# Half of a feed-forward's down-projection blocks computed with seven half-size products, and up and down work interleaved

## The chip, the cores and the metric

The kernel runs on one core of one Trainium2 chip. The metric is the device time of one execution in microseconds, from its first to its last instruction with the launch around it. Five engines run their own instruction streams and meet through semaphores: TensorE (PE in the profile, with PEld for the loads of its stationary operand), VectorE (DVE), ScalarE (ACT), GpSimd (POOL) and SyncE (SP), which only issues the DMAs.

## The reference

A two-layer decoder trunk on a sequence of 256 positions with model width 2048. Each layer has a mixer and then a dense feed-forward with hidden width 8192; the change touches only the two feed-forwards:

```python
def squared_relu_mlp(h, w_up, w_down):
    return jnp.square(jax.nn.relu(h @ w_up)) @ w_down
...
    for layer in range(DEPTH):
        ...
        y = squared_relu_mlp(rmsnorm(h, norm_w[layer, 2]), ffn_w_up[layer], ffn_w_down[layer])
        h = h + rmsnorm(y, norm_w[layer, 3])
```

All tensors are float32.

## The kernel before

**Three products for one.** Every operand is split into a rounded part and a remainder (`whi` and `wlo` for weights, `e0h` and `e0l` for hidden activations), and a product is the sum of three matmuls: high times high, low times high, high times low. A unit of weights is one DMA of 1 MB into a `raw` tile (128 partitions, 2048 columns: four 128-row tiles of 512 columns each). ScalarE then writes `whi` (line 122) and VectorE writes `wlo = raw - whi` (line 123). There are three `raw` buffers and four each of `whi` and `wlo`, so the preparation of a unit can run up to four units ahead of its use.

**A feed-forward.** The hidden width is cut into 16 chunks of 512. The function `first_chunk` computes chunk 0. For each chunk from 1 to 15, `up_pass` computes the hidden chunk transposed: four units, in each unit 48 matmuls with 256 moving columns, into two `tp` banks of PSUM (lines 315 to 317). ScalarE applies relu (line 332), GpSimd squares (line 333), and the result is split into `e` (lines 185 and 186). Then `down` multiplies the hidden chunk before it with the down weights, in four blocks of 512 output columns: per block one unit of weights and 24 matmuls with 512 moving columns, into two `acc` banks, one for each half of the 256 positions. VectorE adds the two banks to `y` in SBUF (line 238) after each block. The order on TensorE is thus four up units, then four down blocks. The last chunk's down projection is done by `down_last`, together with the norm and the residual.

**What sets the order.** The tile framework schedules the instructions onto each engine's queue when the kernel is built; on each engine the order is then fixed, and waits are on semaphores. PSUM has eight banks of 512 float32 columns: four `acc`, two `tp`, two `mx`.

Of the kernel before, what the change touches and what calls it, by code (L numbers as in the profile page):

```python
# [10 lines left out]
F32 = mybir.dt.float32  # L11
# [6 lines left out]
P = 128  # L18
# [13 lines left out]
AHEAD = 200  # L32

# [57 lines left out]
def program(tc, nc, A, S):  # L91
# [60 lines left out]
    def chunk_tok(s, X, rows, spans, n):  # L152
        ps = [bank(acc, n, "acc") for _ in range(2)]
        for u in range(0, len(rows), 4):
            w = weights(s, [(r, spans) for r in rows[u : u + 4]])
            for j in range(4):
                k = u + j
                for b in range(2):
                    prod_tok(ps[b], X[k], b, w, j, n, k == 0, k == len(rows) - 1)
                tick()  # L160
# [142 lines left out]
    def up_pass(s, X, c):  # L303

        ps = [bank(tpp, 512, "tp") for _ in range(2)]
# [13 lines left out]
        return ps  # L319

    def ffn(up, dn, X, rh, w1i, w0i):
        with tc.tile_pool(name=f"ffn{w1i}", bufs=1, reuse_waits="tile") as fp:

            def hidden(e, b, ps):
# [3 lines left out]
                blocks_split(T(fp, [P, 512], "tr", bufs=2), r, e, b)  # L328

            def hidden_t(e, i, ps):  # L330
                r = T(fp, [P, 512], "rl", bufs=3)
                ACT.activation(r, ps, AF.Relu)  # L332
                G.tensor_tensor(r, r, r, ALU.mult)  # L333
                sl = slice(2 * i, 2 * i + 2)
                split(e[0][:, sl, :], e[1][:, sl, :], r.rearrange("p (m t) -> p m t", t=SEQ))
# [4 lines left out]
            e = group(fp, "e0h", "e0l")  # L340
            for b, ps in first_chunk(up, X, [(0, 512)]):
                hidden(e, b, ps)
            for c in range(1, HID // 512):
                e2 = group(fp, f"e{c % 2}h", f"e{c % 2}l")
                ps = up_pass(up, X, c)
                for i in range(2):
                    hidden_t(e2, i, ps[i])
                down(dn, kts([e]), rows(c - 1), c == 1)
                e = e2
            w1 = row_load([T(fp, [P, 512], f"w1{c}") for c in range(4)], "nrow", w1i)  # L350
            w0 = None
            if w0i is not None:
                w0 = row_load([T(fp, [P, 512], f"w0{c}") for c in range(4)], "nrow", w0i)
            return down_last(dn, kts([e]), rows(HID // 512 - 1), w1, w0,
                             lambda b: [T(fp, [P, 512], f"yw{c}") for c in range(4)], rh)
# [662 lines left out]
```

## Time and profile before

| | |
|---|---|
| median of 3 runs (lowest to highest) | 2580.64 us (2579.50 to 2581.19) |
| the profiled execution | 2581.39 us, span 2579.6 us |
| mean granted TensorE clock | 0.996 |
| TensorE busy | 2544.0 us (99%) |
| VectorE, ScalarE, GpSimd busy | 1620.2 us (63%), 1075.3 us (42%), 302.2 us (12%) |
| DMA | 477.85 MB, 185 GB/s in the mean |

The span is the time between the first and the last instruction in the trace; the profiled execution's own time is 1.8 us longer, and 0.75 us above the median. A busy TensorE is not TensorE at its peak, since the recorded matmuls overlap in the pipeline; how far apart they start tells its pace.

### The profile page before, as it was taken

To read this page: it belongs to the slowest core of one execution; us is meant where nothing else is said; L and a number is where in the kernel's file an instruction comes from. 1 tells how busy PE (TensorE), PEld (TensorE's weight loads), DVE (VectorE), ACT (ScalarE), POOL (GpSimd) and SP (SyncE) were. 2 spreads that over 40 slices of the span, in tenths; PEclk is the share of its full clock that TensorE was granted. 3 is DMA by queue.
4 is the path that set the end of the run, shared out by engine and by line. 5 is a ranking of instruction groups with operands and counts; after the bars stand their busy time and mean duration, and the time that the engine had idled before them with its cause. 6 is when DMAs were issued, how large, how long until landed. Compare 5 with 4: busy or idle time off the path is not lost.

```text
span 2579.6 us, 33644 instructions
## 1 busy us (share of the span) xinstructions
PE 2544.0 (99%) x14058; PEld 2183.4 (85%) x14058; DVE 1620.2 (63%) x1774; ACT 1075.3 (42%) x1084; POOL 302.2 (12%) x222
## 2 busy tenths in 40 slices
PE   8999999999999999999999999999999999999998
PEld 7778888879899898989878877777798998989897
DVE  7586855576555656555654596876865555565655
ACT  6555444443434333343443333333534343333433
POOL 3001101140000000000310110110400000000001
PEclk9999999999999999999999999999999999999999
DMA  7544545656555555555455555555465555555553
GB/s 243 177 157 142 196 153 173 209 177 214 193 181 189 187 185 191 182 193 181 156 211 185 175 204 203 190 194 196 163 216 192 181 193 181 190 186 184 191 182 112
DMA packets 81241, 477.85 MB, mean 185 GB/s; under 512 B 13633, under 2 KB 15809, under 8 KB 26817
## 3 DMA queue, kind: packets, MB, share of 16 engines
q1 hardware_dynamic: 81088, 475.70, 53.7%
q8 instruction: 110, 1.80, 0.3%
q14 instruction: 43, 0.34, 0.0%
HBM read 473.04 MB, written 2.62 MB: 184 GB/s over the span
## 4 chain that ended last, share of the span: by engine, by line
PE 48%; DVE 2%; POOL 0%; issue 0%; DVEq 0%; POOLq 0%; ACT 0%; ACTq 0%
PE acc L131 11%; PE acc L129 11%; PE acc L130 11%; PE tp L315 4%; PE tp L316 4%; PE tp L317 4%; DVE h L271 1%; PE mx L928 0%; DVE wlo L123 0%; DVE bc L214 0%; DVE y L259 0%; POOL rs L181 0%; DVE xl L186 0%; POOL e L275 0%; POOL yw L275 0%
## 5 line engine op out<-in xcount | busy, mean ns | idle before, releaser
L123 DVE TENSOR_TENSOR wlo<-raw,whi 128x2048 fp32r<-128x2048 f32 (+2 forms) x440 | 1000.4, 2276 | 729.9 <-ACT whi L122 727.7
L122 ACT ACTIVATE whi<-raw 128x2048 fp32r<-128x2048 f32 (+2 forms) x440 | 828.4, 1883 | 1019.1 <-PE acc L130 604.7
L315 PE MATMUL tp<-xh,whi 128*128 128x256 f32 x1920 | 539.6, 281 | 0.0
L317 PE MATMUL tp<-xh,wlo 128*128 128x256 f32 x1920 | 539.4, 281 | 0.0
L316 PE MATMUL tp<-xl,whi 128*128 128x256 f32 x1920 | 539.4, 281 | 0.0
L129 PE MATMUL acc<-whi,xh 128*128 128x512 f32 (+3 forms) x1120 | 447.1, 399 | 6.1 <-ACT whi L122 6.1
L131 PE MATMUL acc<-wlo,xh 128*128 128x512 f32 (+3 forms) x1120 | 440.1, 393 | 8.6 <-DVE wlo L123 8.6
L130 PE MATMUL acc<-whi,xl 128*128 128x512 f32 (+3 forms) x1120 | 439.5, 392 | 0.0
L316 PEld LDWEIGHTS tp<-xl,whi 128*128 128x128 f32 x1920 | 361.8, 188 | 1.4
L315 PEld LDWEIGHTS tp<-xh,whi 128*128 128x128 f32 x1920 | 361.7, 188 | 1.4
L317 PEld LDWEIGHTS tp<-xh,wlo 128*128 128x128 f32 x1920 | 361.8, 188 | 0.0
L131 PEld LDWEIGHTS acc<-wlo,xh 128*128 128x128 f32 x1120 | 212.0, 189 | 57.3 <-DVE wlo L123 11.0
L129 PEld LDWEIGHTS acc<-whi,xh 128*128 128x128 f32 x1120 | 212.4, 190 | 52.3 <-ACT whi L122 7.0
L130 PEld LDWEIGHTS acc<-whi,xl 128*128 128x128 f32 x1120 | 212.6, 190 | 45.0 <-issue 1.0
L333 POOL TENSOR_TENSOR rl<-rl 128x512 f32<-128x512 f32 x60 | 95.5, 1592 | 1219.3 <-ACT rl L332 1139.1
L238 DVE TENSOR_TENSOR y<-acc,y 128x512 f32<-128x512 f32 x248 | 167.8, 689 | 72.6 <-PE acc L131 71.8
L130 PE MATMUL acc<-whi,e1l 128*128 128x512 f32 x512 | 202.3, 395 | 0.0
L131 PE MATMUL acc<-wlo,e1h 128*128 128x512 f32 x512 | 202.3, 395 | 0.0
L129 PE MATMUL acc<-whi,e1h 128*128 128x512 f32 x512 | 202.3, 395 | 0.0
L130 PE MATMUL acc<-whi,e0l 128*128 128x512 f32 x512 | 202.3, 395 | 0.0
L131 PE MATMUL acc<-wlo,e0h 128*128 128x512 f32 x512 | 202.2, 395 | 0.0
L129 PE MATMUL acc<-whi,e0h 128*128 128x512 f32 x512 | 202.2, 395 | 0.0
(268 smaller groups left out, 2464.7 us busy)
## 6 DMA issues: line engine op xcount, KB each, us to landing
raw<-up SPq DMA_DIRECT2D x128, 1024.0 KB, 4.9
raw<-dn SPq DMA_DIRECT2D x128, 1024.0 KB, 4.9
raw<-sg_in SPq DMA_DIRECT2D x64, 1024.0 KB, 5.0
raw<-la_in SPq DMA_DIRECT2D x56, 1024.0 KB, 5.0
raw<-sg_out SPq DMA_DIRECT2D x32, 1024.0 KB, 5.0
raw<-la_out SPq DMA_DIRECT2D x16, 1024.0 KB, 5.0
raw<-la_in SPq DMA_DIRECT2D x4, 768.0 KB, 4.3
w<-nrow SPq DMA_DIRECT2D x12, 256.0 KB, 5.8
```

Of the source, the lines that this page charges most:

```text
L122: ACT.activation(a, r, AF.Copy)
L123: V.tensor_tensor(d, r, a.bitcast(F32), ALU.subtract)
L129: PE.matmul(ps, xh, wh, start=first, stop=False)
L130: PE.matmul(ps, xl, wh, start=False, stop=False)
L131: PE.matmul(ps, xh, wl, start=False, stop=last)
L238: V.tensor_tensor(y[b][c], ps, y[b][c], ALU.add)
L271: V.scalar_tensor_tensor(ht, yb[c], rs, ht, ALU.mult, ALU.add)
L315: PE.matmul(out, wh[:, col], xh, start=k == 0 and m % 2 == 0, stop=False, skip_group_check=True)
L316: PE.matmul(out, wh[:, col], xl, start=False, stop=False, skip_group_check=True)
L317: PE.matmul(out, wl[:, col], xh, start=False, stop=k == NKT - 1, skip_group_check=True)
L333: G.tensor_tensor(r, r, r, ALU.mult)
```

## The change

**Seven products.** A down block multiplies a 256 x 512 matrix of hidden values by a 512 x 512 matrix of weights. In two of the four blocks (`SEVEN`, output columns 0 to 511 and 1024 to 1535) and for 15 of the 16 chunks, both matrices are cut into halves in each direction, and the product is formed by Winograd's variant of Strassen's scheme from seven products of halves in place of eight. A product of halves is six matmuls with 256 moving columns (two tiles of 128 rows, three matmuls each), so a block has 42 matmuls of 256 columns where it had 24 of 512. The stationary operand is a 128 x 128 tile of `e`, or of `f`, which holds sums and differences of halves of `e`; `sums` forms `f` once for each chunk. The weights' sums are formed by VectorE in `qsum` (four quarter matrices), and both `raw` and `qsum` are split, so such a block takes two `whi` and two `wlo` buffers. Its results fill two `acc` banks (`pa`, `pb`) and two `mx` banks (`pc`, and half of `pd`), each added to an accumulator of its own. `combine` turns the accumulators into `y` after the last such block.

**One block kept.** The block `KEPT` (columns 512 to 1023) accumulates over its 15 chunks in two `acc` banks and is copied out once; two `acc` banks are left for the other blocks.

**Alternation.** `up_pass` is now a generator that stops after each unit. `ORDER` puts one down block behind each up unit (`None` is an up unit); `FIRST` is the order for chunk 1. The rows of the norm weights are loaded into tiles of `f` and `e` that are no longer needed.

```diff
+SEVEN, KEPT = (0, 2), 1
+ORDER = (None, 0, None, 1, None, 2, None, 3)
+FIRST = (None, None, 1, None, 0, None, 3, 2)
...
-    def chunk_tok(s, X, rows, spans, n):
-        ps = [bank(acc, n, "acc") for _ in range(2)]
+    def chunk_tok(s, X, rows, spans, n, ps=None, first=True, last=True):
+        if ps is None:
+            ps = [bank(acc, n, "acc") for _ in range(2)]
...
-                    prod_tok(ps[b], X[k], b, w, j, n, k == 0, k == len(rows) - 1)
+                    prod_tok(ps[b], X[k], b, w, j, n, first and k == 0, last and k == len(rows) - 1)
...
-    def up_pass(s, X, c):
-
-        ps = [bank(tpp, 512, "tp") for _ in range(2)]
...
-        return ps
+            yield
+    def mul7(s, pool, rows, col):
+        H = 256
+        n1, n2 = [(col, H)], [(col + H, H)]
+        src, width = s.take([(rows[0], n2), (rows[1], n2), (rows[0], n1), (rows[1], n1),
+                             (rows[2], n2), (rows[3], n2), (rows[2], n1), (rows[3], n1)])
+        raw = T(wp, [P, 2048], "raw", bufs=RAW_BUFS)
+        q = T(pool, [P, 2048], "qsum")
+        hi = [T(wp, [P, 2048], "whi", F32R, bufs=HI_BUFS) for _ in range(2)]
+        lo = [T(wp, [P, 2048], "wlo", F32R, bufs=LO_BUFS) for _ in range(2)]
+        DMA.dma_start(raw, src)
+        B = raw.rearrange("p (q n) -> p q n", n=512)
+        Q = q.rearrange("p (q n) -> p q n", n=512)
+        V.tensor_tensor(Q[:, 0:2, :], B[:, 1:3, :], B[:, 0:1, :].to_broadcast([P, 2, 512]), ALU.add)
+        V.tensor_tensor(Q[:, 2, :], Q[:, 0, :], B[:, 2, :], ALU.add)
+        V.tensor_tensor(Q[:, 3, :], Q[:, 2, :], B[:, 3, :], ALU.add)
+        split(hi[0][:, :1536], lo[0][:, :1536], raw[:, 512:])
+        split(hi[1], lo[1], q)
+        return [[(t[0][:, k * 512 : (k + 1) * 512], t[1][:, k * 512 : (k + 1) * 512]) for k in range(n)]
+                for t, n in (((hi[0], lo[0]), 3), ((hi[1], lo[1]), 4))]
+    def chunk7(s, pool, e, f, rows, col):
+        (b11, b22, b21), (q1, q3, q2, q4) = mul7(s, pool, rows, col)
+        def plain(half, b):
+            return [[t[:, 2 * half + k, b * P : (b + 1) * P] for t in e] for k in range(2)]
+        def summed(i):
+            return [[t[:, i, k * P : (k + 1) * P] for t in f] for k in range(2)]
+        def prod(ps, x, w):
+            for k in range(2):
+                wh, wl = [t[:, k * 256 : (k + 1) * 256] for t in w]
+                PE.matmul(ps, x[k][0], wh, start=k == 0, stop=False, skip_group_check=True)
+                PE.matmul(ps, x[k][1], wh, start=False, stop=False, skip_group_check=True)
+                PE.matmul(ps, x[k][0], wl, start=False, stop=k == 1, skip_group_check=True)
+        R1, R2, R3, S4 = range(4)
+        pa, pd, pb, pc = bank(acc, 512, "acc"), bank(mxp, 256, "mx"), bank(acc, 512, "acc"), bank(mxp, 512, "mx")
+        prod(pa[:, :256], plain(0, 0), b11)
+        prod(pa[:, 256:], plain(1, 0), b21)
+        prod(pd, summed(S4), b22)
+        prod(pb[:, :256], summed(R2), q2)
+        prod(pb[:, 256:], summed(R3), q3)
+        prod(pc[:, :256], summed(R1), q1)
+        prod(pc[:, 256:], plain(1, 1), q4)
+        return pa, pb, pc, pd
...
+            def sums(a, c):
+                t = T(fp, [P, 1024], "tr")
+                F = t.rearrange("p (i m t) -> p i m t", m=2, t=P)
+                V.tensor_tensor(F[:, 0], a[1][0], a[1][1], ALU.subtract)
+                V.tensor_tensor(F[:, 1], F[:, 0], a[0][0], ALU.subtract)
+                V.tensor_tensor(F[:, 2], a[0][0], a[1][0], ALU.subtract)
+                V.tensor_tensor(F[:, 3], F[:, 1], a[0][1], ALU.add)
+                f = pair(f"f{c % 2}")
+                split(f[0].rearrange("p a t -> p (a t)"), f[1].rearrange("p a t -> p (a t)"), t)
+                return f
...
+            Y, kept = {}, [bank(acc, 512, "acc") for _ in range(2)]
+            def add(key, ps, first, n=512):
+                if first:
+                    Y[key] = T(hp, [P, 512], *BUF[key])[:, :n]
+                    V.tensor_copy(Y[key], ps)
+                else:
+                    V.tensor_tensor(Y[key], ps, Y[key], ALU.add)
...
+            def block(c, g, e, f):
+                if c in SEVEN:
+                    ps = chunk7(dn, fp, e, f, rows(g), c * 512)
+                    for k, p, n in zip("abcd", ps, (512, 512, 512, 256)):
+                        add((k, c), p, g == 0, n)
+                elif c == KEPT:
+                    chunk_tok(dn, kts([e]), rows(g), [(c * 512, 512)], 512, kept, g == 0, g == last - 1)
+                    if g == last - 1:
+                        for b in range(2):
+                            acc_to_y(kept[b], b, c, True)
+                else:
+                    for b, p in enumerate(chunk_tok(dn, kts([e]), rows(g), [(c * 512, 512)], 512)):
+                        acc_to_y(p, b, c, g == 0)
...
+            def combine(c):
+                a, b, p, p3 = [Y[k, c] for k in "abcd"]
+                u = T(fp, [P, 512], "rl", bufs=3)[:, :256]
+                l, r = slice(0, 256), slice(256, 512)
+                V.tensor_tensor(u, a[:, l], b[:, l], ALU.add)
+                V.tensor_tensor(a[:, l], a[:, l], a[:, r], ALU.add)
+                V.tensor_tensor(a[:, r], p[:, l], p3, ALU.add)
+                V.tensor_tensor(a[:, r], a[:, r], u, ALU.subtract)
+                V.tensor_tensor(u, u, b[:, r], ALU.add)
+                V.tensor_tensor(b[:, l], u, p[:, r], ALU.add)
+                V.tensor_tensor(b[:, r], p[:, l], u, ALU.subtract)
+                y[0][c], y[1][c] = a, b
...
-            for c in range(1, HID // 512):
-                e2 = group(fp, f"e{c % 2}h", f"e{c % 2}l")
-                ps = up_pass(up, X, c)
-                for i in range(2):
-                    hidden_t(e2, i, ps[i])
-                down(dn, kts([e]), rows(c - 1), c == 1)
-                e = e2
...
+            for c in range(1, last + 1):
+                e2 = pair(f"e{c % 2}")
+                if c == last:
+                    w1 = row_load(rows_in(["f1h", "f1l"]), "nrow", w1i)
+                ps = [bank(tpp, 512, "tp") for _ in range(2)]
+                todo = up_pass(up, X, c, ps)
+                order = ORDER if c > 1 else FIRST
+                for n, o in enumerate(order):
+                    if o is None:
+                        next(todo)
+                        if None not in order[n + 1 :]:
+                            r = [relu2(p) for p in ps]
+                            for i in range(2):
+                                sl = slice(2 * i, 2 * i + 2)
+                                split(e2[0][:, sl, :], e2[1][:, sl, :], r[i].rearrange("p (m t) -> p m t", t=SEQ))
+                            if c < last:
+                                a = [x.rearrange("p (m b t) -> p b m t", b=2, t=P) for x in r]
+                                f2 = sums([[a[i][:, b] for i in range(2)] for b in range(2)], c)
+                    else:
+                        block(o, c - 1, e, f)
+                e, f = e2, f2
+            for o in SEVEN:
+                combine(o)
```

**VectorE, around the end of an up pass, before.** `wlo` is a weight split, `e0l` the split of the new hidden chunk, `y` the add of a finished `acc` bank.

```order
L123 TENSOR_TENSOR wlo_5490<-raw_5488,whi_5489 128x2048
L186 TENSOR_TENSOR e0l_5155<-rl_5374,e0h_5154 128x512
L186 TENSOR_TENSOR e0l_5155<-rl_5379,e0h_5154 128x512
L238 TENSOR_TENSOR y_923_5042<-acc_5384,y_923_5042 128x512
L238 TENSOR_TENSOR y_924_5044<-acc_5385,y_924_5044 128x512
L123 TENSOR_TENSOR wlo_5526<-raw_5524,whi_5525 128x2048
L238 TENSOR_TENSOR y_930_5078<-acc_5418,y_930_5078 128x512
```

**The same place, now.** `qsum` rows form weight sums, `tr` rows form the sums that become `f`, and lines 190 and 126 are the splits.

```order
L341 TENSOR_TENSOR qsum_6153<-raw_6152 128x1024
L190 TENSOR_TENSOR wlo_6156<-raw_6152,whi_6154 128x1536
L342 TENSOR_TENSOR qsum_6153<-qsum_6153,raw_6152 128x512
L400 TENSOR_TENSOR tr_6051<-rl_6041 128x256
L190 TENSOR_TENSOR e1l_5664<-rl_6041,e1h_5663 128x512
L190 TENSOR_TENSOR e1l_5664<-rl_6044,e1h_5663 128x512
L398 TENSOR_TENSOR tr_6051<-rl_6041,rl_6044 128x256
L343 TENSOR_TENSOR qsum_6153<-qsum_6153,raw_6152 128x512
L399 TENSOR_TENSOR tr_6051<-tr_6051,rl_6041 128x256
L401 TENSOR_TENSOR tr_6051<-tr_6051,rl_6044 128x256
L242 TENSOR_TENSOR y_948_5160<-acc_6060,y_948_5160 128x512
L190 TENSOR_TENSOR wlo_6157<-qsum_6153,whi_6155 128x2048
```

Behind these follow the split `f1l`, the add of the second bank of the plain block (`y_949`) and the split for the next up unit. Between the splits of the hidden chunk and the next weight split there are now the sums for `f`, and the second half of a seven-product block's weights waits there too. The same 33 VectorE rows come for each of the middle chunks of both feed-forwards.

**TensorE, where the first down block of a feed-forward begins, before.** The whole of the up pass for chunk 1 stands ahead of it.

```order
L129 MATMUL acc_5010<-whi_5013,e0h_4612 128x512
L130 MATMUL acc_5010<-whi_5013,e0l_4613 128x512
L131 MATMUL acc_5010<-wlo_5014,e0h_4612 128x512
L129 MATMUL acc_5011<-whi_5013,e0h_4612 128x512
L130 MATMUL acc_5011<-whi_5013,e0l_4613 128x512
```

**TensorE in the same first round, now: the seven-product block that follows directly on a plain block.** The plain block used both free `acc` banks; `acc_5178` is this block's `pa`.

```order
L363 MATMUL mx_5181<-whi_5167,f0l_4788 128x256
L364 MATMUL mx_5181<-wlo_5169,f0h_4787 128x256
L362 MATMUL mx_5181<-whi_5167,f0h_4787 128x256
L362 MATMUL acc_5178<-whi_5166,e0h_4614 128x256
L363 MATMUL acc_5178<-whi_5166,e0l_4615 128x256
```

Ten matmuls into the two `mx` banks now stand between the end of the plain block and the first matmul that needs an emptied `acc` bank. In the later rounds an up unit stands between any two down blocks.

## Rows read from the trace of the kernel before

**Rows 1.** The page: span, TensorE, granted clock in 40 slices.

```profile
span 2579.6 us, 33644 instructions
...
PE 2544.0 (99%) x14058; PEld 2183.4 (85%) x14058; DVE 1620.2 (63%) x1774; ACT 1075.3 (42%) x1084; POOL 302.2 (12%) x222
...
PEclk9999999999999999999999999999999999999999
```

**Rows 2.** Windows, one hidden chunk: busy us (instructions) by engine, clock, DMA share, GB/s.

```profile
876.10:921.20 45.10, 45.10 (x290) 40.70 (x290) 25.74 (x18) 17.43 (x13) 3.19 (x2) 1.00 0.54 187
```

**Rows 3.** Timeline of TensorE over that chunk: start us, us, instruction; cut.

```profile
875.92 0.28 PE L317 MATMUL tp<-xh,wlo 128*128 128x256 f32 x1
876.04 0.39 PE L129 MATMUL acc<-whi,e0h 128*128 128x512 f32 x1
876.28 0.40 PE L130 MATMUL acc<-whi,e0l 128*128 128x512 f32 x1
...
898.21 0.39 PE L131 MATMUL acc<-wlo,e0h 128*128 128x512 f32 x1
898.44 0.28 PE L315 MATMUL tp<-xh,whi 128*128 128x256 f32 x1
...
921.16 0.39 PE L129 MATMUL acc<-whi,e1h 128*128 128x512 f32 x1
```

**Rows 4.** Groups by form, whole span: TensorE 256-wide matmuls and their loads.

```profile
L315 PE MATMUL tp<-xh,whi 128*128 128x256 f32 x1920 | 539.6, 281 | 0.0
...
L317 PEld LDWEIGHTS tp<-xh,wlo 128*128 128x128 f32 x1920 | 361.8, 188 | 0.0
```

**Rows 5.** Groups by form, VectorE: total us, mean ns, idle before.

```profile
L123 DVE TENSOR_TENSOR wlo<-raw,whi 128x2048 fp32r<-128x2048 f32 x424 | 976.1, 2304 | 725.0 <-ACT whi L122 723.6 <-PE acc L131 0.9
...
L123 DVE TENSOR_TENSOR wlo<-raw,whi 128x1024 fp32r<-128x1024 f32 x4 | 4.9, 1227 | 4.7 <-ACT whi L122 4.0 <-PE mx L676 0.7
...
L775 DVE TENSOR_TENSOR bc<-PT 128x256 f32<-128x256 f32 x8 | 3.4, 424 | 5.5 <-POOL PT L773 5.3
```

**Rows 6.** Groups by form, ScalarE.

```profile
L122 ACT ACTIVATE whi<-raw 128x2048 fp32r<-128x2048 f32 x424 | 811.4, 1914 | 1004.8 <-PE acc L130 600.1 <-PE tp L316 319.3 <-DMA raw<-sg_out 44.1
L332 ACT ACTIVATE rl<-tp 128x512 f32<-128x512 f32 x60 | 35.3, 588 | 94.4 <-PE tp L317 94.4
...
L185 ACT ACTIVATE e1h<-rl 128x512 fp32r<-128x512 f32 x32 | 19.9, 623 | 36.1 <-POOL rl L333 36.1
...
L122 ACT ACTIVATE whi<-raw 128x1536 fp32r<-128x1536 f32 x4 | 5.9, 1481 | 5.7 <-DMA raw<-la_in 5.7
...
L122 ACT ACTIVATE whi<-raw 128x1024 fp32r<-128x1024 f32 x4 | 4.2, 1056 | 4.6 <-PE acc L130 4.6
```

**Rows 7.** Timeline of VectorE around the end of an up pass.

```profile
742.71 2.29 DVE L123 TENSOR_TENSOR wlo<-raw,whi 128x2048 fp32r<-128x2048 f32 x1 [3.39 <-ACT whi L122]
744.92 1.53 DVE L186 TENSOR_TENSOR e0l<-rl,e0h 128x512 fp32r<-128x512 f32 x1
746.61 0.69 DVE L186 TENSOR_TENSOR e0l<-rl,e0h 128x512 fp32r<-128x512 f32 x1 [0.15 <-ACT e0h L185]
747.21 1.28 DVE L238 TENSOR_TENSOR y<-acc,y 128x512 f32<-128x512 f32 x2
748.41 2.29 DVE L123 TENSOR_TENSOR wlo<-raw,whi 128x2048 fp32r<-128x2048 f32 x1
```

**Rows 8.** Timeline of GpSimd at the same place.

```profile
740.85 1.04 POOL L333 TENSOR_TENSOR rl<-rl 128x512 f32<-128x512 f32 x1 [40.07 <-ACT rl L332]
743.76 2.15 POOL L333 TENSOR_TENSOR rl<-rl 128x512 f32<-128x512 f32 x1 [1.86 <-ACT rl L332]
```

**Rows 9.** Windows in the last stretch of the first feed-forward.

```profile
1260.00:1280.00 20.00, 18.74 (x85) 14.31 (x83) 13.32 (x20) 9.03 (x15) 8.99 (x8) 1.00 0.26 97
1280.00:1300.00 20.00, 19.23 (x88) 14.93 (x88) 19.26 (x24) 13.64 (x30) 14.76 (x7) 1.00 0.65 236
```

**Rows 10.** The page, DMA issues: count, size, us to landing.

```profile
raw<-dn SPq DMA_DIRECT2D x128, 1024.0 KB, 4.9
```

More of the change, by code (lines that the diff above doesn't have):

```diff
@@ L301, in program, with up_pass @@
     ALLK = [k * P for k in range(NKT)]
-    def up_pass(s, X, c):
-        ps = [bank(tpp, 512, "tp") for _ in range(2)]
+    def up_pass(s, X, c, ps):
         for u in range(4):
@@ L321, in ffn, with pair, relu2 @@
     def ffn(up, dn, X, rh, w1i, w0i):
+        last = HID // 512 - 1
         with tc.tile_pool(name=f"ffn{w1i}", bufs=1, reuse_waits="tile") as fp:
-            def hidden(e, b, ps):
+            def pair(name):
+                return T(fp, [P, 4, SEQ], f"{name}h", F32R), T(fp, [P, 4, SEQ], f"{name}l", F32R)
+            def relu2(ps):
                 r = T(fp, [P, 512], "rl", bufs=3)
@@ L327, in hidden, with rows_in @@
                 G.tensor_tensor(r, r, r, ALU.mult)
[L328 to L335, printed above, removed]
+                return r
+            def rows_in(tags):
+                t = [T(fp, [P, 2, 512], g) for g in tags]
+                return [t[0][:, 0], t[0][:, 1], t[1][:, 0], t[1][:, 1]]
@@ L337, in rows @@
             def rows(c):
                 return [c * 512 + j * P for j in range(4)]
-            e = group(fp, "e0h", "e0l")
-            for b, ps in first_chunk(up, X, [(0, 512)]):
-                hidden(e, b, ps)
-            for c in range(1, HID // 512):
-                e2 = group(fp, f"e{c % 2}h", f"e{c % 2}l")
-                ps = up_pass(up, X, c)
-                for i in range(2):
-                    hidden_t(e2, i, ps[i])
-                down(dn, kts([e]), rows(c - 1), c == 1)
-                e = e2
@@ L350, in ffn @@
[L350 to L355, printed above, removed]
+            Y, kept = {}, [bank(acc, 512, "acc") for _ in range(2)]
[5 more added lines that the diff above has]
+                    V.tensor_tensor(Y[key], ps, Y[key], ALU.add)
@@ new lines, in ffn @@
+            BUF = {("a", 0): ("y00",), ("b", 0): ("y10",), ("a", 2): ("y02",), ("b", 2): ("y12",)}
+            for c in SEVEN:
+                BUF["c", c] = BUF["d", c] = ("bc", F32, 4)
+            def block(c, g, e, f):
[11 more added lines that the diff above has]
+                        acc_to_y(p, b, c, g == 0)
@@ new lines, in halves_of @@
+            def halves_of(tiles):
+                return [[t[:, m] for m in range(2)] for t in tiles]
+            e = pair("e0")
+            t = [T(hp, [P, 512], "bc", bufs=4) for _ in range(2)]
+            for b, ps in first_chunk(up, X, [(0, 512)]):
+                blocks(t[b], relu2(ps))
+                sl = slice(b * P, (b + 1) * P)
+                split(e[0][:, :, sl], e[1][:, :, sl], t[b].rearrange("p (j c) -> p j c", c=P))
+            v = [a.rearrange("p (i m t) -> p i m t", i=2, t=P) for a in t]
@@ new lines, in ffn @@
+            f = sums([[v[b][:, i] for i in range(2)] for b in range(2)], 0)
+            for c in range(1, last + 1):
[19 more added lines that the diff above has]
+                e, f = e2, f2
@@ L357, in layer0_mixer @@
+            for o in SEVEN:
+                combine(o)
+            w0 = None if w0i is None else row_load(rows_in(["f0h", "f0l"]), "nrow", w0i)
+            return down_last(dn, kts([e]), rows(last), w1, w0, lambda b: rows_in(["e0h", "e0l"]), rh)
     def layer0_mixer():
```

## Prediction

> **What bounds the kernel now.** I read the page first: TensorE is busy for 2544.0 of 2579.6 us and its granted clock is in the top tenth in all 40 slices [rows 1], so the time follows the number and spacing of matmuls, and nothing else counts unless TensorE comes to wait for it. Then the windows, for one hidden chunk: TensorE busy 45.10 of 45.10 us, clock 1.00 (the 2.4 GHz level), VectorE 25.74, ScalarE 17.43, GpSimd 3.19 [rows 2]. Then TensorE's timeline over that chunk, by starts, since recorded matmuls overlap: the 96 down matmuls of 512 columns run from 876.04 to 898.44, 0.2333 us each; the 192 up matmuls of 256 columns from 898.44 to 921.16, 0.1183 us each [rows 3]. So a down block (24) takes 5.60 us, an up unit (48) 5.68, a chunk 45.12. Half the columns cost half the time although each matmul loads another stationary tile. The neighbours come last: VectorE's and ScalarE's durations [rows 5, 6] and what they do at the end of an up pass [rows 7, 8].
>
> **The products.** A seven-product block has 42 matmuls of 256 columns: 42 x 0.1183 = 4.97 us for 5.60, a saving of 0.63. Two such blocks, 15 chunks and two feed-forwards make 60: -37.8 us. The chunk becomes 43.85 us. Its matmuls are of the up pass's form (load per matmul, half a bank of PSUM), so I take that spacing; bounds for it stand under the rivals.
>
> **VectorE in a steady chunk.** Per operation I take start-to-start times. Measured: 2.21 for a 2048-column split, 0.60 for an add or a 512-column operation in sequence [rows 7]. For 1024 columns I take 1.15 (its duration is 1.227 [rows 5], and starts of the 2048 split lie 0.1 closer than its duration), for 1536 the mean, 1.68, for 256 columns 0.34 (between half of 0.60 and the 0.424 in [rows 5]). A chunk has 33 operations: eight 2048 splits 17.7, two 1536 splits 3.4, weight sums 2 x 1.15 + 4 x 0.60 = 4.7, adds of the four results 6 x 0.60 + 2 x 0.34 = 4.3, the plain block's adds 1.2, splits of `e` 0.60 + 1.53 = 2.1, four `tr` 1.4, split of `f` 1.15. Sum 35.9 of 43.85 us: 82%, no bound. The trace has no weight sum from a repeated operand and no strided `tr`; from below they cost what I took, from above twice that, as an `e0l` split did once (1.53 against 0.69 [rows 7]): +6.1 per chunk, kept for a rival. ScalarE adds two splits of 1481, a net none of 1914 and one of 1056 ns [rows 6] to its 17.43, about 21.5: covered. Every unit is still one 1 MB DMA, which lands in 4.9 us [rows 10] with three `raw` buffers and units 5.5 us apart: nothing.
>
> **Where a chunk could wait.** The narrow place is the end of an up pass: `e` and `f` of the new chunk must be ready by the next chunk's first seven-product block, and the sums for `f` stand in VectorE's queue ahead of that block's second weight split, the add that frees a bank and the next unit's split. Let 0 be the end of the last up unit. TensorE runs the plain block to 5.60, an up unit to 11.28, then the seven-product block, whose 13th matmul (12.7) is the first to need `f`; its 19th (13.4) needs the bank of `y_949`; the next up unit begins at 16.25.
> VectorE's walk starts when block 2's `pa` is full, at -9.1: add 0.60, split 2.21, adds 0.60, 0.34 and 0.60, split 2.21, `qsum` 1.15, 1536 split 1.68, to +0.3; then `qsum` to 0.9. ScalarE's two relus (0.588 each [rows 6]) end at 0.1 and 0.7. The two squares take 1.04 us alone and 2.15 beside VectorE [rows 8]; at 2.15 each they end at 2.25 and 4.4. `e1h` of the second half (0.623 [rows 6]) ends at 5.0, its `e1l` at 5.6; three `tr` and one `qsum` reach 7.2, the add `y_948` 7.85. ScalarE meanwhile splits `qsum` from 6.6 to 8.5 (1.914), VectorE its remainder to 10.7, then `f1l` to 11.85, `y_949` 12.45, the next unit's split 14.65. Slack is 0.9, 1.0 and 1.6 us. After its backlog VectorE comes to the next `pa` at about 31.6 and waits for it until 34.8, so no lateness carries over: 0 for the 28 such boundaries.
>
> **First round.** Here block 2 follows directly on block 3, which filled both free `acc` banks; ten matmuls cover 1.2 us, so the first bank must be copied out by 5.60 + 1.2 = 6.8 after the up pass. VectorE, from that point: `qsum` to 0.25, squares at 1.2 to 2.25, `tr` and `qsum` to 3.8, a unit's split 6.0, splits of `e` 7.2, `tr` 7.55, copy 8.2. Stall about 1.5, twice: +3.0. Both ends: 0 if the copies are early, 3 each if the squares run at 2.15.
>
> **End.** `combine` is 14 operations, some 5 us of VectorE by 0.34 to 0.42 each, while the last blocks run; the last hidden split is now covered by one block (5.60) where it had four (22.4), and should be ready at 4 to 5.6, needed at 7.0. The old trace already lets TensorE wait there: 18.74 and 19.23 busy of 20 [rows 9]. Nothing to 6 us each; I take 0.5, hence +1.0, because the walk has it in time.
>
> **Sum.** 2581.4 (the profiled execution) - 37.8 + 3.0 + 1.0 = 2547.6; that execution is 0.75 above the median, so 2547 us.
>
> **Rivals.**
> *A wait at the boundary takes back the gain.* The slack of 0.9 us is 4% of a chain of 21 us of VectorE and GpSimd work. For it: every price but the measured ones is interpolated, and the squares and VectorE disturb one another (1.04 to 2.15, 0.69 to 1.53 [rows 7, 8]). Against: I already pay 2.15 for both squares. Each us beyond the slack costs 28 us: 1 us gives 2575. The Trainium skill, page "SBUF — State Buffer", section "Who interferes with whom", says that a VectorE instruction with two SBUF inputs and a GpSimd instruction that reads SBUF shut each other out for its whole length; the trace's two doublings agree. By that rule each square would end earlier or later by where it falls between splits, and my estimate for `f1l` is 10.8 in place of 11.85: the same sum. Chance 0.12.
>
> *VectorE becomes the bound: slower.* The repeated, strided and summing operations cost twice my price, +6.1 us per chunk; 3.2 of it goes into the wait before `pa`, 2.9 stalls TensorE at each boundary: 2547 + 28 x 2.9 = 2628. It decides from +4.4 per chunk, 1.7 times the price (3.2, and 33.8 us of gain over 28). For it: the 1.53 us split. Against: its neighbour of the same form took 0.69 [rows 7], and duration follows columns from 424 ns to 2304 [rows 5]. Chance 0.04.
>
> *Seven products are no saving.* If a product's matmuls went at the pace of their loads, 188 ns [rows 4], a block would take 7.90 us, +2.30 x 60 = +138: 2547 + 38 + 138 = about 2723. Against: the up pass has the same load for each matmul and starts one every 0.118 [rows 3]. The Trainium skill, page "TensorE: Matmul & The Clock Gate", section "Back-to-back issue gap", gives for steady pairs of load and matmul about 81 ns at 128 columns and 131 at 512, so half-width matmuls would cost more than half. My estimate by it, with 98 ns at 256: a block 1.31 times as long, 7.33 us, +104 in all, 2689. This trace shows 0.2333 and 0.1183, a ratio of 1.97, which decides. Chance 0.02.
>
> **How the numbers follow.** The forecast, no stall but in the first round, has 0.80: 2543 (no first-round or end cost: 2581.4 - 37.8 - 0.75) to 2556. The boundary wait has 0.12, the bound on VectorE 0.04, the load pace 0.02, anything else 0.02. What a measurement of this kernel can tell from no change is about 0.2%, 5 us: 2575.5 to 2585.8. The boundary wait stays faster up to 1.0 us of stall (28.5 over 28), which I give half its chance; the rest is split between same and slower. Faster 0.86, same 0.05, slower 0.09. The range for 8 in 10 runs from 2542 to 2568: below, a little for the end's old waits going; above, the end's 6 us each or a boundary stall of 0.7 us.
>
> **What would show it.** In the profile after: down matmuls of lines 362 to 364 starting 0.118 apart, a steady chunk of 43.85 us from one first `pa` matmul to the next, TensorE without idle time between; a hole of 1 to 2 us once per feed-forward after ten matmuls into `mx`; VectorE about 36 us per chunk with a wait of some 3 us ahead of the `pa` add; the weight sums near 1.2 (1024) and 0.6 us. I am wrong on the products if the pitch is above 0.118 or the clock below 1.00; on the boundary if idle time stands before the 13th or 19th matmul of block 0, released by `f1l` or `y_949`; on VectorE's prices if L341 to L343 or L398 to L401 last much beyond 1.2, 0.7 and 0.4 us; on the end if the last 40 us of a feed-forward have more idle TensorE than the old 2.

## The result, and the profile after

The changed kernel takes 2547.43 us (median of 4 runs, 2545.96 to 2548.88) against 2580.07 of the kernel before on the same chip: a ratio of 0.9875, 95% interval 0.9863 to 0.9888. The forecast was 2547. That the total came out so closely is luck: its terms were off by about -4, +12, -6 and -1 us, which nearly cancel. The experiments take them apart. The profiled execution is the slowest of the four, 2548.88 us.

The page of the changed kernel, to be read against [rows 1]:

```profile
span 2547.1 us, 36465 instructions
...
PE 2506.0 (98%) x15138; PEld 2211.3 (87%) x15138; DVE 1968.8 (77%) x2256; ACT 1201.2 (47%) x1174; POOL 285.8 (11%) x222
...
PEclk9999999999999999999999999999999999999999
```

32.5 us of span are gone. TensorE has 1080 more matmuls (60 blocks, 18 more each) and is busy for 38 us less; the rest of its span is idle for 41.1 us where it was for 35.6, so something new waits. VectorE went from 63% to 77%.

TensorE's timeline over one steady chunk (start us, us, instruction; cut), for [rows 3], and the window of that chunk, for [rows 2]:

```profile
841.19 0.39 PE L132 MATMUL acc<-whi,e1h 128*128 128x512 f32 x1
...
846.78 0.28 PE L318 MATMUL tp<-xh,whi 128*128 128x256 f32 x1
...
852.46 0.28 PE L362 MATMUL acc<-whi,e0h 128*128 128x256 f32 x1
...
857.36 0.28 PE L318 MATMUL tp<-xh,whi 128*128 128x256 f32 x1
...
896.16 0.28 PE L362 MATMUL acc<-whi,e1h 128*128 128x256 f32 x1
```

```profile
852.46:896.15 43.69, 43.69 (x326) 41.49 (x325) 37.00 (x35) 21.66 (x15) 2.57 (x2) 1.00 0.52 193
```

The plain block still takes 5.59 us (841.19 to 846.78), the up unit 5.68, the seven-product block 4.90 (852.46 to 857.36): 0.1167 us for each of its 42 matmuls. From one first `pa` matmul to the next are 43.70 us, where a chunk was 45.12, and TensorE has no idle time in it at clock 1.00.

VectorE's timeline around the same boundary (in brackets: idle time ahead, and what ended it), for [rows 7]:

```profile
832.22 0.69 DVE L416 TENSOR_TENSOR y<-acc,y 128x512 f32<-128x512 f32 x1 [3.01 <-PE acc L364]
...
841.55 1.53 DVE L342 TENSOR_TENSOR qsum<-qsum,raw 128x512 f32<-128x512 f32 x1
843.01 1.26 DVE L400 TENSOR_TENSOR tr<-rl 128x256 f32<-128x256 f32 x1
...
847.13 0.68 DVE L242 TENSOR_TENSOR y<-acc,y 128x512 f32<-128x512 f32 x1
848.47 2.29 DVE L190 TENSOR_TENSOR wlo<-qsum,whi 128x2048 fp32r<-128x2048 f32 x1 [0.66 <-ACT whi L189]
850.67 1.22 DVE L190 TENSOR_TENSOR f0l<-tr,f0h 128x1024 fp32r<-128x1024 f32 x1
```

The walk of the prediction is there row for row: the add of `pa` with 3.01 us of idle time ahead (forecast: 3.2), the weight sum L342, the sums for `f`, the add of the plain block, the split of `qsum`, and `f0l`, which ends at 851.89: 10.7 us after the up pass for a forecast of 11.85, and 2.0 us ahead of its need. Two rows are longer than others of their kind: L342 takes 1.53 us and L400 1.26, where 0.69 and 0.41 are usual. They stand beside GpSimd's two squares (841.41 to 843.99 us).

TensorE's largest wait in total, by what ended it (us in total, times, longest):

```profile
PE acc L362 <- DVE y L240: 9.0, 2, 4.5
```

This row is new, two holes of 4.5 us, one in each feed-forward: the first round, where block 2 follows on block 3. TensorE's timeline there, and the windows of the hole and of what follows:

```profile
616.34 0.28 PE L362 MATMUL mx<-whi,f0h 128*128 128x256 f32 x1
...
617.39 0.28 PE L362 MATMUL mx<-whi,f0h 128*128 128x256 f32 x1
622.15 0.58 PE L362 MATMUL acc<-whi,e0h 128*128 128x256 f32 x1 [4.48 <-DVE y L240]
622.52 0.41 PE L363 MATMUL acc<-whi,e0l 128*128 128x256 f32 x1
622.74 0.41 PE L364 MATMUL acc<-wlo,e0h 128*128 128x256 f32 x1
...
627.22 0.30 PE L364 MATMUL acc<-wlo,f0h 128*128 128x256 f32 x1
627.36 0.28 PE L363 MATMUL mx<-whi,f0l 128*128 128x256 f32 x1
...
628.29 0.28 PE L318 MATMUL tp<-xh,whi 128*128 128x256 f32 x1
```

```profile
617.60:622.10 4.50, 0.07 (x1) 0.00 (x0) 4.50 (x7) 0.20 (x1) 0.00 (x0) 0.81 0.21 47
622.10:626.00 3.90, 3.85 (x18) 3.85 (x19) 3.90 (x5) 2.10 (x2) 0.00 (x0) 0.50 0.51 214
626.00:628.60 2.60, 2.60 (x19) 2.60 (x19) 1.56 (x4) 1.04 (x2) 0.00 (x0) 0.76 0.87 347
628.60:632.00 3.40, 3.40 (x31) 3.40 (x31) 3.40 (x4) 1.75 (x1) 0.00 (x0) 1.00 0.11 43
```

The hole is 4.48 us of waiting, and it costs more: the matmuls behind it start 0.21 us apart in place of 0.117, with the granted clock at 0.50 (1.2 GHz) until 627.2. That is 24 matmuls and 2.3 us more. The whole block, 4.90 us elsewhere, takes 11.95 us here (616.34 to 628.29), 7.05 more; in the second feed-forward, with 29 slow matmuls, it takes 12.44 us (1891.86 to 1904.30), 7.54 more. VectorE in the stretch of the first hole:

```profile
611.22 2.88 DVE L190 TENSOR_TENSOR wlo<-qsum,whi 128x2048 fp32r<-128x2048 f32 x1
614.14 1.95 DVE L341 TENSOR_TENSOR qsum<-raw 128x1024 f32<-128x1024 f32 x1
...
621.41 0.69 DVE L240 COPY y<-acc 128x512 f32<-128x512 f32 x1
```

The up pass ended at 610.74. VectorE was then still copying out block 0's results (to 611.22) and had the second split of block 2 to do (2.88 us), so the `qsum` with which my walk began started at 614.14, ended at 616.09, and the copy that frees the bank ended at 622.1. The split and the `qsum` took 2.88 and 1.95 us, where 2.29 and 1.22 are usual; they too stand beside the squares (610.91 to 611.95 and 613.35 to 615.00).

### The profile page after: what moved, and what is told of

The parts are those of the page before. It is cut to its first block, busy times and chain, and to the rows that moved or that the text cites. A ratio compares the mean times of both kernels' runs of the same rounds, so it can differ in the third digit from the quotient of the medians.

```text
span 2547.1 us, 36465 instructions
## 1 busy us (share of the span) xinstructions
PE 2506.0 (98%) x15138; PEld 2211.3 (87%) x15138; DVE 1968.8 (77%) x2256; ACT 1201.2 (47%) x1174; POOL 285.8 (11%) x222
## 3 DMA queue, kind: packets, MB, share of 16 engines
q8 instruction: 119, 1.95, 0.3%
## 4 chain that ended last, share of the span: by engine, by line
PE 45%; DVE 4%; POOL 1%; issue 1%; ACT 0%; DVEq 0%; POOLq 0%; ACTq 0%
PE acc L133 9%; PE acc L134 9%; PE acc L132 9%; PE tp L318 4%; PE tp L319 4%; PE tp L320 4%; PE acc L362 1%; PE acc L364 1%; PE acc L363 1%; DVE wlo L126 1%; PE mx L363 1%; PE mx L362 1%; PE mx L364 1%; DVE h L275 1%; DVE bc L218 1%
## 5 line engine op out<-in xcount | busy, mean ns | idle before, releaser
L126 DVE TENSOR_TENSOR wlo<-raw,whi 128x2048 fp32r<-128x2048 f32 (+3 forms) x380 | 860.3, 2267 | 269.1 <-ACT whi L125 267.1
L125 ACT ACTIVATE whi<-raw 128x2048 fp32r<-128x2048 f32 (+3 forms) x380 | 714.1, 1880 | 566.3 <-PE acc L133 319.2
L132 PEld LDWEIGHTS acc<-whi,xh 128*128 128x128 f32 x1120 | 212.4, 190 | 51.8 <-ACT whi L125 6.3
L387 POOL TENSOR_TENSOR rl<-rl 128x512 f32<-128x512 f32 x64 | 83.0, 1313 | 1261.0 <-ACT rl L386 1136.3
L189 ACT ACTIVATE whi<-qsum 128x2048 fp32r<-128x2048 f32 x60 | 115.3, 1922 | 179.9 <-DVE qsum L343 178.9
L190 DVE TENSOR_TENSOR wlo<-qsum,whi 128x2048 fp32r<-128x2048 f32 x60 | 138.7, 2312 | 79.0 <-ACT whi L189 77.0
L416 DVE TENSOR_TENSOR y<-acc,y 128x512 f32<-128x512 f32 x112 | 76.9, 687 | 86.1 <-PE acc L364 86.1
L189 ACT ACTIVATE whi<-raw 128x1536 fp32r<-128x1536 f32 x60 | 89.6, 1493 | 108.2 <-DMA raw<-dn 79.0
L133 PE MATMUL acc<-whi,e1l 128*128 128x512 f32 x288 | 114.0, 396 | 0.0
L134 PE MATMUL acc<-wlo,e1h 128*128 128x512 f32 x288 | 113.8, 395 | 0.0
L132 PE MATMUL acc<-whi,e1h 128*128 128x512 f32 x288 | 113.7, 395 | 0.0
```

What stands on the lines that cost most here:

```text
L125: ACT.activation(a, r, AF.Copy)
L126: V.tensor_tensor(d, r, a.bitcast(F32), ALU.subtract)
L132: PE.matmul(ps, xh, wh, start=first, stop=False)
L133: PE.matmul(ps, xl, wh, start=False, stop=False)
L134: PE.matmul(ps, xh, wl, start=False, stop=last)
L189: ACT.activation(hi, src, AF.Copy)
```

## Experiments

Each was timed with the kernel before on the same chip; times are medians, and in brackets stands the ratio to the kernel before with its 95% interval. The kernel before took 2579.39 to 2580.07 us on these chips, so times are also compared across them.

**The order of the first round.**

```diff
-FIRST = (None, None, 1, None, 0, None, 3, 2)
+FIRST = (None, None, 1, 0, None, 2, None, 3)
```

> Only the order of the first round changes: the seven-product block 0 stands behind the kept block 1, and an up unit stands again between blocks 2 and 3. Theory 1: the hole of 4.5 us per feed-forward comes from two blocks next to each other that share two free banks while VectorE is behind with its weight splits; it goes, TensorE's waits for the copy fall from 9.0 us to under 1, and the time falls by 7 to 9 us, to about 2539. Rival: VectorE's backlog of the first round is what costs, wherever the blocks stand; then a wait of about the same size shows before block 0 (for f0l or wlo) or before the next unit, and the time stays at 2545 to 2549.

Measured: 2533.27 us (0.982, 0.9807 to 0.9834), 14.1 us under the changed kernel. Theory 1 holds as to the cause, and its size was too small: the 9.0 us of waits fall to 1.1, and with the hole goes the slow clock behind it, which I had not counted. The two blocks had cost 7.05 + 7.54 = 14.6 us too much; less the 1.1, and with the waits for `e0l` (0.8) gone too, that makes 14.3. What is left of the waits in the first rounds of this run:

```profile
PE mx L362 <- DVE bc L414: 1.1, 2, 0.6
```

**The other order of the last two blocks.**

```diff
-FIRST = (None, None, 1, None, 0, None, 3, 2)
+FIRST = (None, None, 1, None, 0, None, 2, 3)
```

> Only the order of the last two blocks of the first round changes: the plain block 3 stands behind the seven-product block 2, still without an up unit between them. Theory 1 (adjacent blocks, two banks, VectorE behind): the plain block needs its second bank 0.7 us after its start, and that bank is full only 1.4 us before, so a hole stays, 1 to 5 us per feed-forward, now ahead of a 512-column matmul; 2540 to 2549. Rival: the seven-product block behind a plain one is special because its sums stand ahead of the copies in VectorE's queue; then the hole goes and the time is about 2538.

Measured: 2544.02 us (0.986, 0.9846 to 0.9873). Theory 1 holds: a hole stays, now ahead of 512-column matmuls, in two pieces:

```profile
619.27 0.47 PE L132 MATMUL acc<-whi,e0h 128*128 128x512 f32 x1 [2.69 <-DVE y L414]
...
623.51 0.50 PE L132 MATMUL acc<-whi,e0h 128*128 128x512 f32 x1 [1.68 <-DVE y L414]
```

```profile
619.20:626.00 6.80, 5.06 (x21) 3.84 (x22) 6.80 (x10) 2.42 (x2) 0.00 (x0) 1.00 0.46 154
```

Its two pieces of 2.69 and 1.68 us sum to nearly the same 4.4 us of waiting per feed-forward, but the clock stays at 1.00 behind them, and the run is 3.4 us faster than the changed kernel.

**Four banks for all blocks.** Block 1 is added up in SBUF too.

```diff
-SEVEN, KEPT = (0, 2), 1
+SEVEN, KEPT = (0, 2), None
...
-            Y, kept = {}, [bank(acc, 512, "acc") for _ in range(2)]
+            Y, kept = {}, None
```

> Block 1 is added to y after each chunk like the other plain block, so four banks serve all blocks and VectorE has two more adds (1.2 us) per chunk. Theory 1: with four banks the hole of the first round goes (-9 us) and the extra adds are hidden, so 2538 to 2540. Rival a: the hole is VectorE's backlog and stays: 2547. Rival b: the adds that the kept block saved are needed; at the end of the up pass the slack of 2 us is used up, and each us more costs 28 us: 2550 to 2575.

Measured: 2541.02 us (0.9848, 0.9835 to 0.9862). Between theory 1 and rival a: the waits for the banks (9.0 us) are gone, and 4.5 us of other waits take their place at the start of the second round, for `whi` and for a split of `qsum`:

```profile
PE acc L364 <- DVE wlo L190: 2.5, 2, 1.3
PE mx L362 <- ACT whi L125: 2.0, 2, 1.0
```

So the hole takes both, the shortage of banks and VectorE's backlog of the first round. What the backlog costs otherwise depends on the order: 4.5 us of waits here, 1.1 in the first experiment. The chunk stays at 43.69 us: rival b falls, and the kept block saves nothing here.

**No seven-product blocks.** Order and kept block stay; the sums are left out.

```diff
-SEVEN, KEPT = (0, 2), 1
+SEVEN, KEPT = (), 1
...
-            f = sums([[v[b][:, i] for i in range(2)] for b in range(2)], 0)
+            f = f2 = None
...
-                            if c < last:
+                            if SEVEN and c < last:
```

> Alternation and the kept block stay, all four blocks are plain (24 matmuls of 512 columns), and no sums are formed. Theory 1: the whole gain comes from fewer matmuls, so a chunk takes 45.1 us again; the time is that of the kernel before, less the 3.5 us of old waits for wlo that went, plus a hole in the first round of 1 to 4 us per feed-forward: 2578 to 2586. Rival: alternation by itself gives a part of the gain, by waits that were hidden in the old order; then 2560 to 2572 and a chunk under 44.8 us.

Measured: 2577.78 us (0.9993, 0.9984 to 1.0002), a hair under the forecast's lower bound. A chunk takes 45.12 us, as before. The whole gain per chunk, 1.43 us, is that of the products; alternation and the kept block give none of it. No run has seven-product blocks without alternation, so what alternation is worth to them is open.

**Loads of the kernel before, moved.** The changed kernel's first up pass begins at 576.85 us, that of the kernel before at 582.60, though the work ahead is the same. Rows of the kernel before: SyncE's wait at the loads of the second layer's norm rows (L915), ScalarE's split that waits for a weight load, TensorE's wait, the window behind it (clock 0.50), and the first matmul of the up pass, followed by that of the changed kernel:

```profile
SPq L915 <- POOL kq L261: 19.3, 1, 19.3
```

```profile
558.73 1.91 ACT L122 ACTIVATE whi<-raw 128x2048 fp32r<-128x2048 f32 x1 [7.08 <-DMA raw<-up]
```

```profile
563.76 0.79 PE L131 MATMUL acc<-wlo,xh 128*128 128x512 f32 x1 [2.32 <-DVE wlo L123]
```

```profile
565.00:570.00 5.00, 4.51 (x15) 3.09 (x15) 4.77 (x9) 3.44 (x9) 3.59 (x3) 0.50 0.88 305
```

```profile
582.60 0.28 PE L315 MATMUL tp<-xh,whi 128*128 128x256 f32 x1
```

```profile
576.85 0.28 PE L318 MATMUL tp<-xh,whi 128*128 128x256 f32 x1
```

The norm rows wait 19.3 us for a `bc` buffer at the head of SyncE's queue, with weight loads behind them. In the changed kernel the `bc` buffers are taken by the feed-forward, so those loads come after it. To test it, the kernel before with four tiny copies in each feed-forward that take the buffers:

```diff
+            for c in range(4):
+                G.tensor_copy(T(hp, [P, 512], "bc", bufs=4)[:, :8], y[0][c][:, :8])
             w1 = row_load([T(fp, [P, 512], f"w1{c}") for c in range(4)], "nrow", w1i)
```

> The kernel before, with one addition: four tiny GpSimd copies into the bc buffers behind the first feed-forward's last chunk, so that the loads of the second layer's norm rows, which stand in SyncE's queue ahead of three weight loads and wait 19.3 us for a buffer there, come after the feed-forward. No matmul changes. Theory: these loads held up the weights at the start of the first feed-forward; TensorE's wait of 2.3 us for wlo and the low clock behind it go, and the time falls by 4 to 6 us, to about 2575. Rival: the eight row loads of the feed-forward itself, which stay, are what delays the weights; then 2578 to 2582.

Measured: 2574.80 us against 2579.44 (0.9983, 0.9974 to 0.9992). The theory holds: the first up pass begins at 577.09, and the clock between 565 and 570 us is 1.00. The gain of 4.6 us belongs to the change, but to a part of the diff that has nothing to do with its products; the run without seven-product blocks has it too (first up pass at 575.48). In the traces of the kernels with this part of the change the up pass begins between 573.85 and 577.63, so 5.75 is the figure of one pair of traces.

**More work for VectorE, at two places.** One weight sum is written again, eight times or four, from the second round on, for block 0 (`col == 0`) or block 2 (`col == 1024`):

```diff
         V.tensor_tensor(Q[:, 3, :], Q[:, 2, :], B[:, 3, :], ALU.add)
+        if col == 0 and rows[0] > 0:
+            for _ in range(8):
+                V.tensor_tensor(Q[:, 3, :], Q[:, 2, :], B[:, 3, :], ALU.add)
```

> The changed kernel, with one weight sum of block 0 (128x512, 0.60 us each) written eight times more from the second round on: 4.8 us more of VectorE per chunk, in the queue between the splits of the new hidden chunk and block 0's second weight split. Theory 1 (what counts is when block 0's operands are ready after the up pass): the last sum ends about 13 us after the up pass, ScalarE's split at 15.1, VectorE's at 17.3, needed at 13.4 and 13.6, so a wait of some 3.6 us at each of 28 boundaries, +100 us, 2640 to 2655. Rival (only VectorE's sum per chunk counts, 37 + 4.8 of 43.7 us): no change, 2545 to 2550.

> The same eight writes (4.8 us per chunk) for block 2, whose sums are formed where VectorE waits for ScalarE and for the next pa by 6 us in all. Theory 1: VectorE comes to the next pa add about 0.6 us late and the boundary has 2 us of slack, so nothing: 2545 to 2550. Rival (any VectorE work is paid, or GpSimd and VectorE share more than the trace shows): as much as the dose at the boundary, or +0.6 x 28 = +17 us.

> The dose for block 2 halved: the weight sum is written four times more, 2.9 us of VectorE per chunk (the eight writes took 5.78 us, not 4.8, and raised the chunk by 1.3 us, the time by 38). Theory now: VectorE's waits in a chunk of the changed kernel are 6.7 us, of which 2.1, the wait for ScalarE's split of the weight sums, cannot be used, so 4.5 us are free; 2.9 fit in and the chunk stays at 43.69 us, the time at 2545 to 2550. Rival: VectorE's work is paid in proportion (1.3 us for 5.78); then +0.65 us per chunk and about 2566.

Measured: 2706.69 us at the boundary (1.0493, 1.0479 to 1.0508), 2585.63 elsewhere (1.0027, 1.0016 to 1.0037), 2545.31 for the half dose there (0.9869, 0.9852 to 0.9885). VectorE's waits between 831 and 1230 us, some 9 chunks: the changed kernel, the full dose for block 2, and the half dose:

```profile
DVE y L416 <- PE acc L364: 28.8, 10, 3.0
DVE wlo L190 <- ACT whi L189: 23.0, 19, 2.1
DVE wlo L126 <- ACT whi L125: 6.8, 8, 0.9
```

```profile
DVE wlo L190 <- ACT whi L189: 18.6, 9, 2.1
```

```profile
DVE wlo L190 <- ACT whi L189: 23.6, 19, 2.1
DVE y L419 <- PE acc L367: 8.8, 8, 1.1
```

At the boundary the mechanism was right and the size too small: each boundary has two stalls, for ScalarE's split of `qsum` and then of the next unit,

```profile
PE acc L365 <- ACT whi L189: 19.7, 9, 2.2
PE tp L318 <- ACT whi L125: 8.1, 8, 1.1
```

the chunk goes to 49.5 us in the mean, and the clock in this stretch is 0.95. The stalls are 3.2 of the 5.8 us more; the slow clock, by estimate 0.05 of 49.5 us, is 2.5, and the expectation had no price for it. Elsewhere neither theory's time came. The eight writes took 5.78 us (0.72 apart in place of 0.60), and the chunk went to 44.9; that makes 34 of the 38 us over the changed kernel, and 4 more come between the two feed-forwards. The count that fits is of VectorE's queue: its idle time fell from 6.7 us a chunk (the three rows and two small ones, 61.4 us over 9.13 chunks) to 2.2, nearly all of it the wait for ScalarE's split of the weight sums; 4.5 us were absorbed and the other 1.3 are the longer chunk. The half dose, 2.9 us, fits in and costs nothing, with the chunk at 43.69. So VectorE has 4.5 us per chunk to spare, and at the boundary about 2.

**Three seven-product blocks.** Block 3 too, with the better first round (two more accumulators in SBUF):

```diff
-SEVEN, KEPT = (0, 2), 1
+SEVEN, KEPT = (0, 2, 3), 1
...
-FIRST = (None, None, 1, None, 0, None, 3, 2)
+FIRST = (None, None, 1, 0, None, 2, None, 3)
```

> Block 3 by seven products too, with the order of the first round that put block 0 behind block 1 (2533.3 us with two such blocks). TensorE needs 0.69 us less per chunk, VectorE 5.0 us more: 42.1 of 43.0 us. Theory 1: VectorE has waits for ScalarE inside a chunk that it cannot avoid (2.7 us), so it becomes the bound; the chunk takes 44 to 45 us, 2540 to 2570. Rival: the waits give way and TensorE stays the bound; 43.0 us per chunk, 2533 - 20 = 2513.

Measured: 2558.12 us (0.9916, 0.9901 to 0.9931). The time is in the theory's range, the chunk a little under it: 43.92 us for TensorE's 43.0. But the chunk, 0.23 us longer than with two such blocks, is only some 6 of the 25 us over the best two-block order; 7 more lie in the second rounds (47.5 and 47.2 us), 6 between the feed-forwards and 6 behind the second. VectorE's and TensorE's waits over the same stretch:

```profile
DVE wlo L190 <- ACT whi L189: 17.3, 9, 2.1
```

```profile
PE acc L364 <- DVE wlo L190: 5.9, 9, 0.8
```

VectorE waits for almost nothing but ScalarE's split, and TensorE waits for VectorE in each chunk.

**Squares on ScalarE**, with the better first round:

```diff
-                G.tensor_tensor(r, r, r, ALU.mult)
+                ACT.activation(r, r, AF.Square)
```

> The order of the first round of the fastest kernel so far (2533.3 us, block 0 behind block 1), and the squares of the hidden chunk on ScalarE in place of GpSimd. Theory (GpSimd's squares hold up VectorE instructions with two inputs in SBUF): the weight sum of 512 columns and the strided sum that meet the squares fall from 1.5 and 1.26 us to 0.69 and 0.41, VectorE is busy some 1.5 us less per chunk, and since it was hidden the time stays within 2 us of 2533. Rival: these two are long for another reason (their operands); then they stay as long.

Measured: 2531.90 us (0.9813, 0.9800 to 0.9827), the fastest kernel of the study, not to be told from the 2533.27 without this edit. The theory holds: VectorE is busy 325.5 us between 831 and 1230 us where it was 339.3 with the squares on GpSimd, 1.5 us less per chunk. The two groups of VectorE rows, first of the changed kernel, then of this run (total us, mean ns, idle before):

```profile
L342 DVE TENSOR_TENSOR qsum<-qsum,raw 128x512 f32<-128x512 f32 x60 | 63.1, 1052 | 0.1
...
L400 DVE TENSOR_TENSOR tr<-rl 128x256 f32<-128x256 f32 x28 | 33.5, 1198 | 0.0
```

```profile
L342 DVE TENSOR_TENSOR qsum<-qsum,raw 128x512 f32<-128x512 f32 x60 | 41.0, 683 | 0.1
...
L400 DVE TENSOR_TENSOR tr<-rl 128x256 f32<-128x256 f32 x28 | 11.7, 417 | 0.0
```

**Three blocks, the kept one last**, without and with the squares on ScalarE:

```diff
-SEVEN, KEPT = (0, 2), 1
+SEVEN, KEPT = (0, 1, 2), 3
...
-FIRST = (None, None, 1, None, 0, None, 3, 2)
+FIRST = (None, None, 3, 0, None, 1, None, 2)
```

> Seven products for blocks 0, 1 and 2, and the last block of each round is the kept one, so that no results are added at the end of an up pass and the last round ends without them. With block 3 as the third one the time was 2558.1 us and VectorE had no free time but one wait of 2.07 us in a chunk of 43.92. Theory: VectorE stays the bound (the same work per chunk but for two adds, 1.2 us), 42.9 to 43.7 us per chunk, and the end costs less; 2520 to 2540. Rival: order at the boundary was the limit; then TensorE's 43.0 us are reached, 2513 to 2518.

> As the run with three seven-product blocks and the kept block last, and the squares on ScalarE. Theory (VectorE is the bound there, and GpSimd's squares lengthen its work by 1.5 us): the chunk comes to TensorE's 43.0 us and the time to 2513 to 2520, under the run with the squares on GpSimd. Rival: the wait for ScalarE's split inside the block is the limit and ScalarE now has more to do; no gain over that run, or a loss.

Measured: 2551.07 us (0.9891, 0.9877 to 0.9904) and 2595.24 (1.0062, 1.0049 to 1.0074). The first time lies outside what either theory gave; the second is the loss that the rival allowed. In the first run the middle chunks do reach TensorE's 43.0 us, with no idle time on TensorE (window with busy us by engine, clock, DMA):

```profile
831.00:1230.00 399.00, 399.00 (x3177) 388.72 (x3176) 378.05 (x360) 210.74 (x148) 36.52 (x18) 1.00 0.55 199
```

VectorE has the same instructions per chunk as with block 3 as the third, so the order at the boundary was a limit there. But the gain is lost elsewhere, most of it in the early rounds: from up pass to up pass, rounds 2 to 4 take 51.8, 46.6 and 44.6 us, 14 us more per feed-forward than three of 43.0. TensorE's longest waits there are for VectorE's split of `qsum` (10.1 us over both feed-forwards, the longest 3.4); what brings them about was not tried. Another 6.6 us lie between the feed-forwards: from the last up pass of the first to the first of the second are 624.6 us where the best two-block order has 618.1. In the second run the chunk takes 45.0 us: ScalarE's split of `qsum` waits for a `whi` buffer that an up unit still holds, and the next up unit then waits for its own:

```profile
ACT whi L189 <- PE tp L319: 61.8, 8, 7.7
```

```profile
PE tp L318 <- ACT whi L125: 9.6, 9, 1.1
```

A seven-product block takes two of the four `whi` buffers. But in the first run, with as many blocks and buffers, ScalarE had this wait once in 399 us (0.8 us), so the number of blocks alone does not make the buffers bind; in the second run ScalarE's splits also stand in another order. Whether a fifth buffer or the old order would free it was not tried.

## Why the prediction was right, and where it was not

**The products (forecast -37.8 us): right, too small.** A block takes 4.90 us in place of 5.60, 0.70 saved and not 0.63, so 60 blocks make -41.9. I took the spacing of the up pass, 0.1183 us [rows 3]; within a seven-product block it is 0.1167, half of the 0.2333 of a 512-column matmul. The run without such blocks shows that nothing else shortens the chunk. The rival by which loads set the pace is out, and so is the pace that the Trainium skill gives on the page "TensorE: Matmul & The Clock Gate", section "Back-to-back issue gap", where half-width matmuls cost more than half: here they cost half.

**VectorE and the boundary (forecast 0): right.** VectorE's 36 us were 37.0 in the window of the chunk, the 3.2 us of free time ahead of `pa` 3.01, and the slack 2.0 where I had 0.9. The two squares took 2.58 us together and not 2.15 each; the hold-up shows on VectorE's side instead, 0.84 us in L342 and 0.85 in L400. With the squares on ScalarE both fall to 0.68 and 0.42. That is the case of the Trainium skill's page "SBUF — State Buffer", section "Who interferes with whom" (a VectorE instruction with two inputs in SBUF and a GpSimd one that reads SBUF shut each other out); this trace agrees, both have two inputs in SBUF. By that rule I had 10.8 us for `f1l`; it came at 10.7. By my own sign (0.7 and 0.4 us) the prices of these two rows were wrong, but VectorE had the time to spare. The rival in which VectorE becomes the bound was to decide from 4.4 us more per chunk: 5.78 us more take the chunk to 44.9 and 2.9 are free. With a third seven-product block TensorE waits for VectorE in each chunk in one order (43.92 us) and not in the other (43.0), so VectorE's work alone is no bound there yet.

**The first round (forecast +3.0): the step that failed.** It read "VectorE, from that point: `qsum` to 0.25": I started the walk as in a steady chunk, with VectorE caught up. In the first round it had the copies of block 0's results and block 2's second split still to do, and that `qsum` ended 5.3 us after the up pass; 1.3 us of this is the hold-up beside the squares. The walk had VectorE wait for the squares later on; these waits did not come, which took back some 1.9 us. So the copy ended at 11.4 in place of 8.2 us, and the hole is 4.5 us each and not 1.5. And I gave no price to what a hole does to the clock, 2.3 us in the first feed-forward and 2.8 in the second. Together +14.6, by the time that the two blocks took; the order that avoids it gives back 14.1.

**The end (forecast +1.0): nothing.** From the last up pass of the first feed-forward to the first of the second, less the down blocks still to come (22.4 and 5.6 us), are 612.5 us before and 612.5 after.

**What I left out:** -5.75 us ahead of the first feed-forward, from loads that leave the head of SyncE's queue. The diff shows it (`bc` buffers for accumulators), but I did not look for what waits on those buffers.

The sum of what was measured, with the new waits for `e0l` (0.8): -41.9 + 14.6 - 5.75 + 0.8 = -32.2, for a span that fell by 32.5. The mechanism of the main term was right; that the total was hit to 0.4 us was luck, since the first round's miss was paid by the loads that I had not seen and by the products.

## What to carry to other kernels

When TensorE is the bound and its matmuls follow each other without a gap, count columns and take the spacing from rows of the same form; here that gave the saving to within a tenth. What decides beside it are the edges: walk the first round from where the vector engine really stands there, not from the steady state, and price a hole by its length and by the slow clock that can stand behind it. A change of buffers moves loads too: list every tile whose buffers change owner, and look for what stood in the DMA queue behind it.

## What the runs showed of the hardware

A hole of 4.48 us on TensorE was followed by some 5 us at 1.2 GHz (granted clock 0.50), while holes of 2.69 and 1.68 us with matmuls between them left it at 1.00. The length of a hole does not decide: one of 2.39 us (three seven-product blocks, block 3 the third) and two of 0.99 and 1.26 us near each other (four banks for all blocks) were followed by a stretch at 0.50. The Trainium skill, page "TensorE: Matmul & The Clock Gate", section "Part 1: The HAM clock gate", says that the clock follows how busy TensorE has lately been; these rows agree in that each slow stretch stands behind a hole, but they do not tell which holes bring one.

Matmuls of 256 columns start 0.1183 us apart in the up pass and 0.1167 in the seven-product blocks, in the same run. What makes the 1.4% was not tried.

On VectorE an instruction that depends on the one before it (the second 512-column weight sum on the first, or the repeated writes of one) starts 0.72 us after it, where independent ones of the same size start 0.60 apart.
